# A matmul with bias and residual: x transposed by VectorE in 32 x 32 blocks of word pairs, instead of by TensorE

## The chip, the cores and the metric

The kernel runs on one core of a Trainium2 chip. The time is device time in microseconds; the kernel before takes 211.29 us (median of three runs, 211.21 to 211.32). Engines are named as the profile names them: PE (TensorE; PEld is its weight load), DVE (VectorE), ACT (ScalarE), POOL (GpSimd) and SP (SyncE, whose queue issues nearly all DMAs here).

## The reference

```python
# x: (16, 512, 1024), weight: (1024, 768), bias: (768,), residual: (16, 512, 768), all float32
return (np.matmul(x, weight) + bias + residual).astype(np.float32)
```

As two-dimensional arrays x is 8192 x 1024, the weights 1024 x 768 and the result 8192 x 768. The kernel multiplies in bf16 and adds in float32.

## The kernel before, in words

The 8192 rows are 64 tiles of 128 rows, in eight groups of G = 8 tiles. A group is loaded whole: partition p gets eight consecutive rows (4 MB of x, 3 MB of residual), and tile j of the group is row j of each partition. x has two slots of a group (`x_tile`); residuals, results and the staged weights share four homes of 3 MB (`home`, in the order of `HOME`).

A tile t goes through these steps:

- `cast_x(t)` (L120): ACT casts the 128 x 1024 tile to bf16, `xb`. It runs three tiles ahead.
- `transpose(t)` (L135): TensorE multiplies eight 128 x 128 pieces of `xb` with an identity into PSUM, `pt`. Piece (h, j) takes every fourth column of a half.
- `copy_xt(t)` (L142): DVE copies `pt` to SBUF, `xt`.
- `matmul(t)` (L149): for each of eight k, one matmul of 512 and one of 256 columns, into `po` in PSUM (three buffers).
- `evacuate(t)` (L163, L166): DVE adds `po` to the residual in place, and POOL adds the bias (L173). In group 0 the residual is not there yet: DVE adds the bias into `o_tile`, and POOL (two of them DVE) later adds the residual (L177).

The order on each engine is the program's order (`keep_in_program_order`). In the main loop PE does the transposes of tile t + 1 and then the product of tile t. All loads of x and residual and all stores are issued from the SP queue in program order; the table `moves` says behind which tile each one stands. An issue waits until its buffer is free and, because there are eight DMA semaphores in turn, until the eighth DMA before it has landed; whatever stands behind it on SP waits too. Ahead of the loop the weights come in four pieces, cast by ACT and DVE alternately, and 14 matmuls on constants (`fill`, L199) keep PE running while the first data arrive. The last tile is done in two column chunks and stored in two pieces.

Of the kernel before, what the change touches and what calls it, by code (L numbers as in the profile page):

```python
# [8 lines left out]
FP32 = mybir.dt.float32  # L9
BF16 = mybir.dt.bfloat16  # L10
P = 128
G = 8
X_BUFS = 2
HOME = [3, 1, 0, 3, 1, 2, 0, 3]
XB_BUFS = 5
XT_BUFS = 4
PT_BUFS = 2
PO_BUFS = 3
# [3 lines left out]
def kernel(  # L22
# [8 lines left out]
    nc = tc.nc  # L31
# [5 lines left out]
    n_k = K // P  # L37
    n_sub = M // P
    n_grp = n_sub // G
    chunks = [(0, 512), (512, N - 512)]  # L40

    def group(ap, g):

        return ap[g * G * P:(g + 1) * G * P, :].rearrange("(p j) k -> p j k", p=P)


    w_dram = weight.rearrange("(h p j) n -> h p j n", p=P, j=4)

# [5 lines left out]
    pt_pool = ctx.enter_context(  # L54
        tc.tile_pool(name="ptp", bufs=1, space=bass.MemoryType.PSUM))
# [3 lines left out]
    def o(ins):  # L59
        return tc.keep_in_program_order(ins)  # L60
# [7 lines left out]


    warm_in = const.tile([P, P], BF16, name="warm_in")  # L70
    o(nc.vector.memset(warm_in, 0.5))
# [5 lines left out]
    ident = const.tile([P, P], BF16, name="ident")  # L77
    make_identity(nc, ident)
    w_sb = const.tile([P, n_k, N], BF16, name="w_sb")
    bias_bc = const.tile([P, N], FP32, name="bias_bc")  # L80

    def home(i, name):
        return ring_pool.tile([P, G, N], FP32, name=name, tag=f"ring{i}", bufs=1)


    x_tiles, r_tiles, o_tiles, w_stage = {}, {}, {}, {}
# [6 lines left out]
    def load_w(h, j0, j1):  # L93
        if not w_stage:
            w_stage[0] = home(0, "w_stage")
        o(nc.sync.dma_start(out=w_stage[0][:, 4 * h + j0:4 * h + j1, :],
                            in_=w_dram[h, :, j0:j1, :]))

    def load_r(g):
        r_tiles[g] = home(HOME[g], "r_tile")  # L100
        o(nc.sync.dma_start(out=r_tiles[g], in_=group(res2d, g)))

    def store(g, j0=0, j1=G, n0=0, n1=N):
        src = o_tiles[g] if g == 0 else r_tiles[g]
        o(nc.sync.dma_start(out=group(out2d, g)[:, j0:j1, n0:n1], in_=src[:, j0:j1, n0:n1]))


    xb_tiles, pt_tiles, xt_tiles, po_tiles = {}, {}, {}, {}

    def cast_x(t, split=False):  # L110
        if t >= n_sub:
            return
        xb_tiles[t] = slot(xb_pool, "xb", XB_BUFS, [P, K], BF16)
        src = x_tiles[t // G][:, t % G, :]
        if split:
            h = K // 2
            o(nc.scalar.copy(out=xb_tiles[t][:, :h], in_=src[:, :h]))  # L117
            o(nc.vector.tensor_copy(out=xb_tiles[t][:, h:], in_=src[:, h:]))  # L118
        else:
            o(nc.scalar.copy(out=xb_tiles[t], in_=src))  # L120

    def cast_w(k, act=False):
        if act:
            o(nc.scalar.copy(out=w_sb[:, k, :], in_=w_stage[0][:, k, :]))  # L124
        else:
            o(nc.vector.tensor_copy(out=w_sb[:, k, :], in_=w_stage[0][:, k, :]))  # L126

    def transpose(t):
        if t >= n_sub:
            return  # L130
        xb = xb_tiles.pop(t).rearrange("m (h p j) -> m h j p", p=P, j=4)
        pt = slot(pt_pool, "pt", PT_BUFS, [P, n_k, P], BF16)
        for k in range(n_k):
            h, j = divmod(k, 4)
            o(nc.tensor.transpose(out=pt[:, k, :], in_=xb[:, h, j, :], identity=ident))  # L135
        pt_tiles[t] = pt

    def copy_xt(t):
        if t >= n_sub:
            return  # L140
        xt_tiles[t] = slot(xt_pool, "xt", XT_BUFS, [P, n_k, P], BF16)
        o(nc.vector.tensor_copy(out=xt_tiles[t], in_=pt_tiles.pop(t)))  # L142

    def matmul(t, k0=0, k1=n_k):
        if t not in po_tiles:
            po_tiles[t] = slot(po_pool, "po", PO_BUFS, [P, N], FP32)
        for k in range(k0, k1):
            for (n0, nl) in chunks:
                o(nc.tensor.matmul(  # L149
                    po_tiles[t][:, n0:n0 + nl],  # L150
                    lhsT=xt_tiles[t][:, k, :],
                    rhs=w_sb[:, k, n0:n0 + nl],
                    start=(k == 0),
                    stop=(k == n_k - 1),
                ))

    def evacuate(t):


        g, j = divmod(t, G)  # L160
        po = po_tiles.pop(t)
        if g == 0:
            o(nc.vector.tensor_add(out=o_tiles[0][:, j, :], in0=po, in1=bias_bc))  # L163
        else:
            rt = r_tiles[g][:, j, :]
            o(nc.vector.tensor_add(out=rt, in0=po, in1=rt))  # L166
            if t < n_sub - 3:
                add_bias(t)
        xt_tiles.pop(t)

    def add_bias(t, engine=nc.gpsimd):
        rt = r_tiles[t // G][:, t % G, :]
        o(engine.tensor_add(out=rt, in0=rt, in1=bias_bc))  # L173

    def add_residual(t, engine=nc.gpsimd):
        ot = o_tiles[0][:, t, :]
        o(engine.tensor_add(out=ot, in0=ot, in1=r_tiles[0][:, t, :]))  # L177


    load_x(0, 0, 2)  # L180
    load_w(0, 0, 2)
    load_x(0, 2, 4)
    for q, n0, n1 in [(0, 0, 512), (0, 512, N), (32, 0, N), (64, 0, N), (96, 0, N)]:
        o(nc.scalar.dma_start(out=bias_rows[q:q + 1, n0:n1], in_=bias[None, n0:n1]))  # L184
    load_w(0, 2, 4)
    load_w(1, 0, 2)
    load_w(1, 2, 4)
    load_x(0, 4, 6)
    load_x(0, 6, 8)
# [3 lines left out]


    warm_ps = po_pool.tile([P, 4, P], FP32, name="warm_ps", tag="po2", bufs=1)

    def fill(n):
        for i in range(n):
            o(nc.tensor.matmul(warm_ps, lhsT=warm_in,  # L199
                               rhs=warm_in[:, None, :].to_broadcast([P, 4, P]),  # L200
                               start=True, stop=True))


    fill(11)
    cast_x(0, True)
    transpose(0)
    fill(2)
    copy_xt(0)
    cast_x(1)
    cast_w(0, True)  # L210
    transpose(1)
    copy_xt(1)
    cast_w(1)
    fill(1)
    matmul(0, 0, 1)
    matmul(1, 0, 1)
    matmul(0, 1, 2)
    matmul(1, 1, 2)
    cast_x(2, True)
    transpose(2)  # L220
    copy_xt(2)
    matmul(2, 0, 2)
    for k in range(2, 6):
        cast_w(k, k % 2 == 0)
        for t in range(3):
            matmul(t, k, k + 1)
    o(nc.vector.stream_shuffle(out=bias_bc, in_=bias_rows, mask=[0] * 32))  # L227
    cast_w(6)
    cast_w(7, True)
    cast_x(3, True)  # L230
    matmul(0, 6, 8)
    evacuate(0)
    transpose(3)
    matmul(1, 6, 8)
    copy_xt(3)
    matmul(2, 6, 8)
    evacuate(1)
    evacuate(2)
    cast_x(4)
    cast_x(5)  # L240
# [3 lines left out]
        4: [(load_x, 2)],  # L244
        5: [(load_r, 0), (load_r, 2)],
        12: [(load_x, 3)],
        15: [(store, 1)],
        17: [(load_r, 3)],
        20: [(load_x, 4)],
        21: [(load_r, 4), (store, 0)],  # L250
        28: [(load_x, 5)],
        29: [(load_r, 5), (store, 2)],
        36: [(load_x, 6)],
        37: [(load_r, 6), (store, 3)],
        44: [(load_x, 7)],
        45: [(load_r, 7), (store, 4)],
        47: [(store, 5)],
        55: [(store, 6)],
        59: [(store, 7, 0, 4)],
        61: [(store, 7, 4, 6)],  # L260
        62: [(store, 7, 6, 7)],
    }
    for t in range(3, n_sub - 1):
        cast_x(t + 3)
        if t == 3:
            matmul(t, 0, 5)
            transpose(t + 1)
            matmul(t, 5, 8)
        elif t == G - 1:
            matmul(t, 0, 2)  # L270
            transpose(t + 1)
            matmul(t, 2, 8)
        else:
            transpose(t + 1)
            matmul(t)
        copy_xt(t + 1)
        if t in (2 * G, 2 * G + 1):
            add_residual(t - 2 * G, nc.vector)
        evacuate(t)
        if t in (n_sub - 9, n_sub - 7, n_sub - 5):  # L280
            add_bias(n_sub - 3 + (t - n_sub + 9) // 2)
        if t == 2 * G - 1:
            for u in range(2, G):
                add_residual(u)
        for move, *what in moves.get(t, []):
            move(*what)


    t = n_sub - 1
    for (n0, nl) in chunks:  # L290
        ps = slot(po_pool, "po", PO_BUFS, [P, nl], FP32, name="last_ps")
        for k in range(n_k):
            o(nc.tensor.matmul(ps, lhsT=xt_tiles[t][:, k, :], rhs=w_sb[:, k, n0:n0 + nl],  # L293
                               start=(k == 0), stop=(k == n_k - 1)))
        rt = r_tiles[n_grp - 1][:, G - 1, n0:n0 + nl]
        o(nc.vector.tensor_add(out=rt, in0=ps, in1=rt))  # L296
        store(n_grp - 1, G - 1, G, n0, n0 + nl)
# [28 lines left out]
```

## Time and profile before

| | before |
|---|---|
| median of 3 runs | 211.29 us (211.21 to 211.32) |
| the profiled execution | 210.92 us, with a span of 209.1 us |
| granted TensorE clock | 1.000 |
| moved by DMA | 87.28 MB, 417 GB/s over the span |
| PE / DVE / ACT / POOL busy | 199.5 / 107.3 / 67.7 / 114.4 us |
| waits of POOL for DVE's sums | 85.2 us |
| SP's waits on POOL before stores | 54.8 us, 3 times |

The span runs from the first to the last instruction of the profiled execution; the time of the execution is 1.82 us longer. Busy time counts the instructions of an engine, with matmuls modelled as pipelined. A row of the groups reads: line, engine, operation, output<-input with shapes, count, then busy time and mean duration in ns, then the idle time just before and what ended it. A row of the windows reads: stretch and length, busy time (and instructions) of PE, PEld, DVE, ACT and POOL, then the granted clock, the share of time in which the DMA engines were busy, and GB/s.

### The profile page before, as it was taken

To read this page: it belongs to the slowest core of one execution; us is meant where nothing else is said; L and a number is where in the kernel's file an instruction comes from. 1 tells how busy PE (TensorE), PEld (TensorE's weight loads), DVE (VectorE), ACT (ScalarE), POOL (GpSimd) and SP (SyncE) were. 2 spreads that over 40 slices of the span, in tenths; PEclk is the share of its full clock that TensorE was granted. 3 is DMA by queue.
4 is the path that set the end of the run, shared out by engine and by line. 5 is a ranking of instruction groups with operands and counts; after the bars stand their busy time and mean duration, and the time that the engine had idled before them with its cause. 6 is when DMAs were issued, how large, how long until landed. Compare 5 with 4: busy or idle time off the path is not lost.

```text
span 209.1 us, 3593 instructions
## 1 busy us (share of the span) xinstructions
PE 199.5 (95%) x1520; PEld 130.8 (63%) x1550; DVE 107.3 (51%) x142; ACT 67.7 (32%) x70; POOL 114.4 (55%) x69
## 2 busy tenths in 40 slices
PE   7679999999999999999999999999999999999992
PEld 2346766666666666666666666666666666666661
DVE  0457555455478545454554554455445445544542
ACT  2446309507331074303632063310733018320000
POOL 2000000365579999966556655655665565599820
PEclk9999999999999999999999999999999999999999
DMA  6999999999999999999999999999999999999994
GB/s 241 416 424 445 461 418 412 464 400 437 431 453 396 418 439 395 454 445 414 431 431 445 418 414 451 434 426 429 417 432 431 461 409 423 417 434 442 409 385 192
DMA packets 5066, 87.28 MB, mean 417 GB/s; under 512 B 565, under 2 KB 694, under 8 KB 1594
## 3 DMA queue, kind: packets, MB, share of 16 engines
q1 hardware_dynamic: 5040, 87.03, 97.8%
q8 instruction: 12, 0.20, 0.4%
q14 instruction: 4, 0.03, 0.0%
q10 hardware_dynamic: 10, 0.01, 0.0%
HBM read 61.88 MB, written 25.17 MB: 416 GB/s over the span
## 4 chain that ended last, share of the span: by engine, by line
PE 82%; DMA 14%; ACT 1%; issue 1%; SPq 0%; DVE 0%; ACTq 0%
PE po L149 69%; PE pt L135 12%; DMA x_tile<-in_x_dram 11%; DMA bias_rows<-in_bias_dram 2%; PE last_ps L293 1%; ACT L76 1%; ACT xb L120 1%; SPq L91 0%; DVE r_tile L296 0%; ACT warm L76 0%; ACTq L120 0%; ACTq L184 0%
## 5 line engine op out<-in xcount | busy, mean ns | idle before, releaser
L149 PE MATMUL po<-w_sb,xt 128*128 128x256 bf16 (+1 forms) x978 | 172.1, 324 | 2.6 <-DVE xt L142 0.8
L173 POOL TENSOR_TENSOR r_tile<-r_tile,bias_bc 128x768 f32<-128x768 f32 x56 | 101.0, 1814 | 85.2 <-DVE r_tile L166 85.2
L149 PEld LDWEIGHTS <-xt 128*128 128x128 bf16 x1008 | 95.8, 98 | 58.9 <-DVE xt L142 1.4
L120 ACT CAST xb<-x_tile 128x1024 bf16<-128x1024 f32 x61 | 61.2, 1044 | 108.5 <-DMA x_tile<-in_x_dram 64.6
L166 DVE TENSOR_TENSOR r_tile<-po,r_tile 128x768 f32<-128x768 f32 x55 | 52.7, 958 | 79.1 <-PE po L149 73.2
L142 DVE COPY xt<-pt 128x1024 bf16<-128x1024 bf16 x64 | 43.6, 682 | 3.1 <-PE pt L135 3.1
L135 PEld LDWEIGHTS <-xb 128*128 128x128 bf16 x512 | 35.4, 113 | 11.0 <-ACT xb L117 3.0
L135 PE MATMUL pt<-ident,xb 128*128 128x128 bf16 x512 | 39.1, 219 | 2.2 <-ACT xb L117 2.2
L177 POOL TENSOR_TENSOR o_tile<-o_tile,r_tile 128x768 f32<-128x768 f32 x6 | 12.1, 2056 | 0.0
L163 DVE TENSOR_TENSOR o_tile<-po,bias_bc 128x768 f32<-128x768 f32 x8 | 7.6, 955 | 7.0 <-PE po L149 7.0
L199 PE MATMUL warm_ps<-warm_in 128*128 128x512 bf16 x14 | 5.3, 530 | 1.0 <-DVE warm L75 1.0
L124 ACT CAST w_sb<-w_stage 128x768 bf16<-128x768 f32 x4 | 3.3, 832 | 3.7 <-DMA w_stage<-in_weight_dram 3.7
L118 DVE CAST xb<-x_tile 128x512 bf16<-128x512 f32 x3 | 1.3, 424 | 6.0 <-DMA x_tile<-in_x_dram 6.0
L199 PEld LDWEIGHTS <-warm_in 128*128 128x128 bf16 x14 | 1.7, 131 | 3.4 <-issue 2.4
L117 ACT CAST xb<-x_tile 128x512 bf16<-128x512 f32 x3 | 1.8, 615 | 5.6 <-DMA x_tile<-in_x_dram 5.6
L177 DVE TENSOR_TENSOR o_tile<-o_tile,r_tile 128x768 f32<-128x768 f32 x2 | 3.3, 1647 | 0.0
L126 DVE CAST w_sb<-w_stage 128x768 bf16<-128x768 f32 x4 | 2.2, 556 | 1.7 <-DMA w_stage<-in_weight_dram 1.7
L293 PE MATMUL last_ps<-w_sb,xt 128*128 128x512 bf16 (+1 forms) x16 | 2.8, 326 | 0.0
L293 PEld LDWEIGHTS <-xt 128*128 128x128 bf16 x16 | 1.6, 98 | 1.1
L296 DVE TENSOR_TENSOR r_tile<-last_ps,r_tile 128x512 f32<-128x512 f32 (+1 forms) x2 | 1.1, 558 | 0.9 <-PE last_ps L293 0.8
L76 ACT ACT_TABLE_LOAD x1 | 1.3, 1283 | 0.7 <-PEq L310 0.7
L227 DVE STREAM_SHUFFLE bias_bc<-bias_rows 128x768 f32<-128x768 f32 x1 | 1.0, 1006 | 0.0
(11 smaller groups left out, 2.1 us busy)
## 6 DMA issues: line engine op xcount, KB each, us to landing
x_tile<-in_x_dram SPq DMA_DIRECT2D x7, 4096.0 KB, 29.2
r_tile<-in_residual_dram SPq DMA_DIRECT2D x8, 3072.0 KB, 17.7
out_dram<-r_tile SPq DMA_DIRECT2D x6, 3072.0 KB, 23.9
x_tile<-in_x_dram SPq DMA_DIRECT2D x4, 1024.0 KB, 8.8
w_stage<-in_weight_dram SPq DMA_DIRECT2D x4, 768.0 KB, 6.5
out_dram<-o_tile SPq DMA_DIRECT2D x1, 3072.0 KB, 31.2
out_dram<-r_tile SPq DMA_DIRECT2D x1, 1536.0 KB
out_dram<-r_tile SPq DMA_DIRECT2D x1, 768.0 KB, 5.5
```

The lines of the kernel that those rows point to most:

```text
L76: o(nc.scalar.copy(out=warm, in_=warm))
L120: o(nc.scalar.copy(out=xb_tiles[t], in_=src))
L124: o(nc.scalar.copy(out=w_sb[:, k, :], in_=w_stage[0][:, k, :]))
L135: o(nc.tensor.transpose(out=pt[:, k, :], in_=xb[:, h, j, :], identity=ident))
L142: o(nc.vector.tensor_copy(out=xt_tiles[t], in_=pt_tiles.pop(t)))
L149: o(nc.tensor.matmul(po_tiles[t][:, n0:n0 + nl], lhsT=xt_tiles[t][:, k, :], rhs=w_sb[:, k, n0:n0 + nl], start=(k == 0), stop=(k == n_k - 1),))
L163: o(nc.vector.tensor_add(out=o_tiles[0][:, j, :], in0=po, in1=bias_bc))
L166: o(nc.vector.tensor_add(out=rt, in0=po, in1=rt))
L173: o(engine.tensor_add(out=rt, in0=rt, in1=bias_bc))
L177: o(engine.tensor_add(out=ot, in0=ot, in1=r_tiles[0][:, t, :]))
L199: o(nc.tensor.matmul(warm_ps, lhsT=warm_in, rhs=warm_in[:, None, :].to_broadcast([P, 4, P]), start=True, stop=True))
L293: o(nc.tensor.matmul(ps, lhsT=xt_tiles[t][:, k, :], rhs=w_sb[:, k, n0:n0 + nl], start=(k == 0), stop=(k == n_k - 1)))
```

## The change

TensorE no longer transposes. `xb` is seen as 32-bit words, each a pair of neighbouring bf16 values, and DVE transposes 32 x 32 blocks of such words. Work goes by batches of B = 4 tiles. The columns of x are split in four quarters q of 256 (128 words); word 4a + j of quarter q is to land on partition 32q + a, so that partition p holds columns 8p to 8p + 7, and the weights are loaded accordingly in one DMA, partition p holding rows 8p to 8p + 7. A transposed block comes out on the 32 partitions its rows were on (m), and must move to the 32 partitions of its quarter (q):

- Quarters 0 and 1: DVE transposes all 128 partitions in one instruction into `tq` (`transpose_blocks`), and ACT moves the blocks in four copies of 32 partitions each (`move_blocks`).
- Quarters 2 and 3: DVE transposes each 32 partitions with an instruction of its own that also writes them to their place (`transpose_and_move`, four instructions).

The product reads every second bf16 of `xt` as weights. There are two `xt` and four `po`; each `xb` quarter and `tq` has one buffer. The identity, the PSUM tiles for transposes, the warming matmuls, the split of the first casts and of the last tile go. All eight residual adds of group 0 are on POOL. The last residual group is loaded into a slot of x, and the order of homes and `moves` is new, now by batches.

The diff, cut to its core:

```diff
-    def transpose(t):
-        xb = xb_tiles.pop(t).rearrange("m (h p j) -> m h j p", p=P, j=4)
-        pt = slot(pt_pool, "pt", PT_BUFS, [P, n_k, P], BF16)
-        for k in range(n_k):
-            h, j = divmod(k, 4)
-            o(nc.tensor.transpose(out=pt[:, k, :], in_=xb[:, h, j, :], identity=ident))
-        pt_tiles[t] = pt
-    def copy_xt(t):
-        xt_tiles[t] = slot(xt_pool, "xt", XT_BUFS, [P, n_k, P], BF16)
-        o(nc.vector.tensor_copy(out=xt_tiles[t], in_=pt_tiles.pop(t)))
+    def load_r(g):
+        if g == n_grp - 1:
+            xs = slot(xin_pool, "x_tile", X_BUFS, [P, G * K], FP32, name="r_last")
+            r_tiles[g] = xs[:, :G * N].rearrange("p (j n) -> p j n", n=N)
+        else:
+            r_tiles[g] = home(HOME[g], "r_tile")
+        o(nc.sync.dma_start(out=r_tiles[g], in_=group(res2d, g)))
+    def cast_x(b, q):
+        g, j = divmod(b * B, G)
+        xb = slot(xb_pool, f"xb{q}_", 1, [P, B, KQ], BF16)
+        o(nc.scalar.copy(out=xb, in_=x_tiles[g][:, j:j + B, q * KQ:(q + 1) * KQ]))
+        xb_tiles[b, q] = xb.bitcast(U32).rearrange("p t (a j) -> p t j a", j=R // 2)
+    def xt_tile(b):
+        if b not in xt_tiles:
+            xt_tiles[b] = slot(xt_pool, "xt", 2, [P, B, R // 2, P], U32)
+        return xt_tiles[b]
+    def transpose_blocks(b, q):
+        tq_tiles[b, q] = slot(xt_pool, f"tq{q}_", 1, [P, B, R // 2, Q], U32)
+        o(nc.vector.transpose(out=tq_tiles[b, q], in_=xb_tiles.pop((b, q))))
+    def move_blocks(b, q):
+        xt, tq = xt_tile(b), tq_tiles.pop((b, q))
+        for m in range(P // Q):
+            o(nc.scalar.copy(out=xt[q * Q:(q + 1) * Q, :, :, m * Q:(m + 1) * Q],
+                             in_=tq[m * Q:(m + 1) * Q]))
+    def transpose_and_move(b, q):
+        xt, xb = xt_tile(b), xb_tiles.pop((b, q))
+        for m in range(P // Q):
+            o(nc.vector.transpose(out=xt[q * Q:(q + 1) * Q, :, :, m * Q:(m + 1) * Q],
+                                  in_=xb[m * Q:(m + 1) * Q]))
     def matmul(t):
+        b, i = divmod(t, B)
+        xt = xt_tiles[b].bitcast(BF16)[:, i].rearrange("p j (m r) -> p j r m", r=2)
...
-                    lhsT=xt_tiles[t][:, k, :],
+                    lhsT=xt[:, k // 2, k % 2, :],
...
+    load_x(0, 0, B)
+    w_stage = home(3, "w_stage")
+    o(nc.sync.dma_start(out=w_stage, in_=weight.rearrange("(p r) n -> p r n", p=P)))
+    load_x(0, B, G)
+    load_x(1)
+    load_r(1)
...
+    load_x(2)
+    load_r(0)
+    load_r(2)
+    moves = {
+        1: [(load_x, 3)],
+        3: [(load_x, 4), (load_r, 3)],
+        4: [(store, 1)],
+        5: [(load_x, 5), (load_r, 4), (store, 0)],
+        7: [(load_x, 6), (load_r, 5), (store, 2)],
+        9: [(load_x, 7), (load_r, 6)],
+        11: [(load_r, 7), (store, 3), (store, 4)],
+        12: [(store, 5)],
+        14: [(store, 6)],
+    }
+    for b in range(n_bat):
+        t = B * b
+        matmul(t)
+        for q in (0, 1):
+            transpose_blocks(b + 1, q)
+        evacuate(t - 1)
+        for q in (0, 1):
+            move_blocks(b + 1, q)
+        for q in range(4):
+            if q < 2:
+                cast_x(b + 2, q)
+        matmul(t + 1)
+        transpose_and_move(b + 1, 2)
+        evacuate(t)
+        cast_x(b + 2, 2)
+        matmul(t + 2)
+        transpose_and_move(b + 1, 3)
+        evacuate(t + 1)
+        cast_x(b + 2, 3)
+        matmul(t + 3)
+        evacuate(t + 2)
+        if b in (2, 3):
+            for u in range(B * (b - 2), B * (b - 1)):
+                add_residual(u)
...
+        if b == n_bat - 1:
+            store(n_grp - 1, 0, B)
+        for move, *what in moves.get(b, []):
+            move(*what)
+    evacuate(n_sub - 1)
+    store(n_grp - 1, B, B + 2)
+    store(n_grp - 1, B + 2, G)
```

In the text below, x3 or r3 is the load of x or of the residual for group 3.

More of the change, by code (lines that the diff above doesn't have):

```diff
@@ L5 @@
 from concourse import mybir
-from concourse.masks import make_identity
 from concourse._compat import with_exitstack
@@ L10 @@
 BF16 = mybir.dt.bfloat16
+U32 = mybir.dt.uint32
 P = 128
+Q = 32
 G = 8
+B = 4
 X_BUFS = 2
[L14 to L18, printed above, removed]
+HOME = [0, 1, 3, 0, 1, 2, 3]
+PO_BUFS = 4
 @with_exitstack
@@ L36 @@
     N = weight.shape[1]
-    n_k = K // P
+    R = K // P
+    KQ = K // 4
     n_sub = M // P
     n_grp = n_sub // G
+    n_bat = n_sub // B
     chunks = [(0, 512), (512, N - 512)]
@@ L44, in group @@
         return ap[g * G * P:(g + 1) * G * P, :].rearrange("(p j) k -> p j k", p=P)
-    w_dram = weight.rearrange("(h p j) n -> h p j n", p=P, j=4)
     const = ctx.enter_context(tc.tile_pool(name="const", bufs=1))
@@ L53 @@
     xt_pool = ctx.enter_context(tc.tile_pool(name="xtp", bufs=1))
-    pt_pool = ctx.enter_context(
-        tc.tile_pool(name="ptp", bufs=1, space=bass.MemoryType.PSUM))
     po_pool = ctx.enter_context(
@@ L67, in slot, with home @@
         return pool.tile(shape, dtype, name=name or base, tag=f"{base}{i % n}", bufs=1)
-    warm_in = const.tile([P, P], BF16, name="warm_in")
-    o(nc.vector.memset(warm_in, 0.5))
+    def home(i, name):
+        return ring_pool.tile([P, G, N], FP32, name=name, tag=f"ring{i}", bufs=1)
     bias_rows = const.tile([P, N], FP32, name="bias_rows")
@@ L76 @@
     o(nc.scalar.copy(out=warm, in_=warm))
-    ident = const.tile([P, P], BF16, name="ident")
-    make_identity(nc, ident)
-    w_sb = const.tile([P, n_k, N], BF16, name="w_sb")
+    w_sb = const.tile([P, R, N], BF16, name="w_sb")
     bias_bc = const.tile([P, N], FP32, name="bias_bc")
-    def home(i, name):
-        return ring_pool.tile([P, G, N], FP32, name=name, tag=f"ring{i}", bufs=1)
-    x_tiles, r_tiles, o_tiles, w_stage = {}, {}, {}, {}
+    x_tiles, r_tiles, o_tiles = {}, {}, {}
     def load_x(g, j0=0, j1=G):
@@ L91, in load_x @@
         o(nc.sync.dma_start(out=x_tiles[g][:, j0:j1, :], in_=group(x2d, g)[:, j0:j1, :]))
[L93 to L97, printed above, removed]
-    def load_r(g):
-        r_tiles[g] = home(HOME[g], "r_tile")
+    def load_r(g):
+        if g == n_grp - 1:
[3 more added lines that the diff above has]
+            r_tiles[g] = home(HOME[g], "r_tile")
@@ L101, in load_r, with store @@
         o(nc.sync.dma_start(out=r_tiles[g], in_=group(res2d, g)))
-    def store(g, j0=0, j1=G, n0=0, n1=N):
+    def store(g, j0=0, j1=G):
         src = o_tiles[g] if g == 0 else r_tiles[g]
[L105 to L111, printed above, removed]
+        o(nc.sync.dma_start(out=group(out2d, g)[:, j0:j1, :], in_=src[:, j0:j1, :]))
+    xb_tiles, tq_tiles, xt_tiles, po_tiles = {}, {}, {}, {}
@@ L112, in cast_x @@
+    def cast_x(b, q):
+        if b >= n_bat:
             return
[L113 to L126, printed above, removed]
@@ L128, in transpose @@
-    def transpose(t):
-        if t >= n_sub:
-            return
-        xb = xb_tiles.pop(t).rearrange("m (h p j) -> m h j p", p=P, j=4)
-        pt = slot(pt_pool, "pt", PT_BUFS, [P, n_k, P], BF16)
-        for k in range(n_k):
-            h, j = divmod(k, 4)
-            o(nc.tensor.transpose(out=pt[:, k, :], in_=xb[:, h, j, :], identity=ident))
-        pt_tiles[t] = pt
-    def copy_xt(t):
-        if t >= n_sub:
-            return
-        xt_tiles[t] = slot(xt_pool, "xt", XT_BUFS, [P, n_k, P], BF16)
-        o(nc.vector.tensor_copy(out=xt_tiles[t], in_=pt_tiles.pop(t)))
@@ L144, in matmul @@
[L144 to L147, printed above, removed]
+        g, j = divmod(b * B, G)
[6 more added lines that the diff above has]
+        return xt_tiles[b]
@@ new lines, in transpose_blocks @@
+    def transpose_blocks(b, q):
+        if b >= n_bat:
+            return
+        tq_tiles[b, q] = slot(xt_pool, f"tq{q}_", 1, [P, B, R // 2, Q], U32)
+        o(nc.vector.transpose(out=tq_tiles[b, q], in_=xb_tiles.pop((b, q))))
+    def move_blocks(b, q):
+        if b >= n_bat:
+            return
+        xt, tq = xt_tile(b), tq_tiles.pop((b, q))
+        for m in range(P // Q):
+            o(nc.scalar.copy(out=xt[q * Q:(q + 1) * Q, :, :, m * Q:(m + 1) * Q],
+                             in_=tq[m * Q:(m + 1) * Q]))
@@ new lines, in transpose_and_move, with matmul @@
+    def transpose_and_move(b, q):
+        if b >= n_bat:
+            return
+        xt, xb = xt_tile(b), xb_tiles.pop((b, q))
+        for m in range(P // Q):
+            o(nc.vector.transpose(out=xt[q * Q:(q + 1) * Q, :, :, m * Q:(m + 1) * Q],
+                                  in_=xb[m * Q:(m + 1) * Q]))
+    def matmul(t):
+        b, i = divmod(t, B)
+        xt = xt_tiles[b].bitcast(BF16)[:, i].rearrange("p j (m r) -> p j r m", r=2)
+        po_tiles[t] = slot(po_pool, "po", PO_BUFS, [P, N], FP32)
+        for k in range(R):
@@ L150, in matmul @@
                     po_tiles[t][:, n0:n0 + nl],
-                    lhsT=xt_tiles[t][:, k, :],
+                    lhsT=xt[:, k // 2, k % 2, :],
                     rhs=w_sb[:, k, n0:n0 + nl],
                     start=(k == 0),
-                    stop=(k == n_k - 1),
+                    stop=(k == R - 1),
                 ))
     def evacuate(t):
+        if t < 0:
+            return
         g, j = divmod(t, G)
@@ L166, in evacuate, with add_bias, add_residual @@
             o(nc.vector.tensor_add(out=rt, in0=po, in1=rt))
-            if t < n_sub - 3:
+            if t < n_sub - 2:
                 add_bias(t)
-        xt_tiles.pop(t)
-    def add_bias(t, engine=nc.gpsimd):
+    def add_bias(t):
         rt = r_tiles[t // G][:, t % G, :]
-        o(engine.tensor_add(out=rt, in0=rt, in1=bias_bc))
-    def add_residual(t, engine=nc.gpsimd):
+        o(nc.gpsimd.tensor_add(out=rt, in0=rt, in1=bias_bc))
+    def add_residual(t):
         ot = o_tiles[0][:, t, :]
[L177 to L189, printed above, removed]
+        o(nc.gpsimd.tensor_add(out=ot, in0=ot, in1=r_tiles[0][:, t, :]))
+    for p in range(0, P, Q):
+        o(nc.scalar.dma_start(out=bias_rows[p:p + 1, :], in_=bias[None, :]))
+    load_x(0, 0, B)
+    w_stage = home(3, "w_stage")
+    o(nc.sync.dma_start(out=w_stage, in_=weight.rearrange("(p r) n -> p r n", p=P)))
+    load_x(0, B, G)
     load_x(1)
@@ L192 @@
     o_tiles[0] = home(2, "o_tile")
[L195 to L240, printed above, removed]
-    moves = {
[L244 to L261, printed above, removed]
-    }
@@ L263 @@
[L263 to L278, printed above, removed]
-        evacuate(t)
[L280 to L283, printed above, removed]
-                add_residual(u)
-        for move, *what in moves.get(t, []):
-            move(*what)
@@ L289 @@
[L289 to L297, printed above, removed]
+    o(nc.vector.stream_shuffle(out=bias_bc, in_=bias_rows, mask=[0] * 32))
@@ new lines @@
+    for q in range(4):
+        cast_x(0, q)
+    for q in (0, 1):
+        transpose_blocks(0, q)
+    for q in (2, 3):
+        transpose_and_move(0, q)
+    for q in (0, 1):
+        move_blocks(0, q)
+    for k in range(R):
+        if k % 2:
+            o(nc.scalar.copy(out=w_sb[:, k, :], in_=w_stage[:, k, :]))
+        else:
+            o(nc.vector.tensor_copy(out=w_sb[:, k, :], in_=w_stage[:, k, :]))
+    for q in range(4):
+        cast_x(1, q)
+    load_x(2)
+    load_r(0)
+    load_r(2)
@@ new lines @@
+    moves = {
+        1: [(load_x, 3)],
[7 more added lines that the diff above has]
+        14: [(store, 6)],
+    }
+    for b in range(n_bat):
+        t = B * b
+        matmul(t)
+        for q in (0, 1):
+            transpose_blocks(b + 1, q)
+        evacuate(t - 1)
+        for q in (0, 1):
+            move_blocks(b + 1, q)
+        for q in range(4):
+            if q < 2:
+                cast_x(b + 2, q)
+        matmul(t + 1)
+        transpose_and_move(b + 1, 2)
+        evacuate(t)
+        cast_x(b + 2, 2)
[7 more added lines that the diff above has]
+            for u in range(B * (b - 2), B * (b - 1)):
+                add_residual(u)
+        if b == n_bat - 3:
+            for u in (n_sub - 2, n_sub - 1):
+                add_bias(u)
+        if b == n_bat - 1:
+            store(n_grp - 1, 0, B)
+        for move, *what in moves.get(b, []):
+            move(*what)
```

## The prediction

> **What bounds the kernel now.** I read the engine and DMA lines of the page first.
>
> ```profile
> PE 199.5 (95%) x1520; PEld 130.8 (63%) x1550; DVE 107.3 (51%) x142; ACT 67.7 (32%) x70; POOL 114.4 (55%) x69
> DMA  6999999999999999999999999999999999999994
> DMA packets 5066, 87.28 MB, mean 417 GB/s; under 512 B 565, under 2 KB 694, under 8 KB 1594
> PE 82%; DMA 14%; ACT 1%; issue 1%; SPq 0%; DVE 0%; ACTq 0%
> ```
>
> Two resources are full at once: TensorE is busy 95% of the span, and the DMA engines are busy in every slice but the first and the last. The chain names PE only because a transfer that arrives in time leaves no wait behind. So I asked for the rates by stretch.
>
> ```profile
> 0.00:6.00 6.00, 4.29 (x11) 1.45 (x11) 0.44 (x3) 1.75 (x3) 1.38 (x7) 1.00 0.70 259
> 6.00:12.00 6.00, 4.01 (x35) 2.25 (x35) 2.61 (x6) 2.74 (x4) 0.00 (x0) 1.00 1.01 419
> ...
> 125.00:150.00 25.00, 24.79 (x194) 16.56 (x196) 12.67 (x17) 8.80 (x9) 15.11 (x9) 1.00 1.00 429
> ...
> 200.00:209.10 9.10, 5.40 (x36) 3.12 (x34) 3.54 (x5) 0.00 (x0) 0.14 (x1) 1.00 0.67 271
> ```
>
> The last two columns are DMA share and GB/s. From 6 to 200 us the share is 1.00 and the weighted rate of all the stretches is 429 GB/s (83.26 MB in 194 us). The first 6 us move 1.55 MB, worth 3.6 us at that rate, and lose 2.4; the last 9.1 us move 2.47 MB, worth 5.75, and lose 3.35. All of the span is then 87.28 MB / 429 = 203.4, plus 2.4, plus 3.35 = 209.1 us. The change moves the same bytes, so freeing TensorE can win back only what lies in the 3.35. Everything else can only be lost. That is the main point of this forecast. Then the groups and two rows of the timeline give durations.
>
> ```profile
> L166 DVE TENSOR_TENSOR r_tile<-po,r_tile 128x768 f32<-128x768 f32 x55 | 52.7, 958 | 79.1 <-PE po L149 73.2
> L142 DVE COPY xt<-pt 128x1024 bf16<-128x1024 bf16 x64 | 43.6, 682 | 3.1 <-PE pt L135 3.1
> L117 ACT CAST xb<-x_tile 128x512 bf16<-128x512 f32 x3 | 1.8, 615 | 5.6 <-DMA x_tile<-in_x_dram 5.6
> L227 DVE STREAM_SHUFFLE bias_bc<-bias_rows 128x768 f32<-128x768 f32 x1 | 1.0, 1006 | 0.0
> L177 DVE TENSOR_TENSOR o_tile<-o_tile,r_tile 128x768 f32<-128x768 f32 x2 | 3.3, 1647 | 0.0
> 35.73 2.60 PE po L149 x16
> 38.33 0.45 PE pt L135 x8
> ```
>
> A tile is 2.60 us of product and 0.45 us of transpose on PE, a period of 3.05.
>
> **TensorE, step by step.** The 512 transposes go: 64 x 0.45 = 29 us. What stays is 64 x 2.60 = 166 us, 10.4 us for a batch of four tiles. The weights of the product are now read with a step of two bf16 words. The trace has a longer step already: L135 loads xb with a step of four words, eight loads in 0.56 us, 70 ns each, while the shorter of the two matmuls of a k lasts 108 (a third of the 325 ns pair). I price the step at nothing. The 14 warming matmuls go too; the first tile may then run slowly for 2 to 3 us, which DMA hides.
>
> **VectorE.** It loses 43.6 us of copies (L142) and some smaller things. It gains, for each batch, two 128 x 512 block transposes and eight of 32 x 512, all of 32-bit words. No row shows a block transpose. The nearest is the shuffle, 1006 ns for 768 words. Two DVE widths of the same add (692 ns for 512, 425 for 256) differ by 1.04 ns a word, so the shuffle is 800 ns of streaming and 206 fixed, and a 512-word transpose 533 + 206 = 0.74 us. Lower end: 0.69, the 512-wide add. Upper end, from the slowest DVE row, L177: (1647 - 206) / 768 = 1.88 ns a word, 1.17 us. I take 0.74, since the shuffle is the row that also moves data between partitions. Two adds back to back on DVE take 1.81 us where their durations sum to 1.91, so the wide pair gets 1.4. The narrow ones each start in another group of 32 partitions, and I give them no overlap: 8 x 0.74 = 5.9. Four evacuations are 3.8. A batch is 11.1 us of DVE, more than PE's 10.4 but less than the 12.7 us that DMA needs for a sixteenth of its 203.4. DVE passes DMA when a transpose takes 0.9 us.
>
> **ScalarE.** Four casts of 1.04 and eight moves of 512 words by L117's 0.615: 4.2 + 4.9 = 9.1 us a batch. It has 2 us of cover under DVE. Its last cast of a batch waits for the last transposes of the batch ahead; behind it on the queue stand the moves of the next batch, which wait for two transposes that come 2.6 us later anyway.
>
> **Start.** The first x load is now 2.1 MB and ends at about 2.4 + 4.9 + 0.8 = 8.1 us, weights at 15.4. Casts 8.1 to 12.1, DVE transposes to about 17, weight casts to 20: the products begin near 17.5 instead of 8.5. The second batch is transposed by about 30, the third by 41, then one each 11.1 us: the sixteenth starts at 41 + 13 x 11.1 = 185, and its last tile is evacuated at 197 if nothing waits. That is before DMA can be done. The late start costs nothing while loads are queued: 14.7 MB are issued without a wait, which keeps DMA busy until 37 us, and the next 10.5 MB are released by the casts of the first eight tiles, near 25.
>
> **The SP queue.** I followed it as first come, first served at 429 GB/s (4.19 MB 9.8 us, 3.15 MB 7.3). x3 ends at 71, x4 (released at 64) at 81. Next is r3, which reuses the home of r0, and r0 is free when POOL has added all eight residual rows. POOL's adds of rows 0 to 3 stand behind tiles 8 to 10 (ready at 49 to 55), and take 4 x 2.06; then four bias adds of 1.81 and four more residual adds. That ends at 80 to 83 us; behind the waiting r3 on SP stand the store of group 1 and x5. The queue runs dry at 81, and from the first issue to first data the trace has about 1.7 us (0.73 to 2.4). I charge 1.9 us of idle DMA, between nothing and 5. In the kernel before, two of these residual adds ran on DVE. After that the releases come 5 to 14 us ahead of need (x5 at 86 for 96, x6 at 108 for 120, x7 at 130 for 145, r7 at 152 for 162). r6 arrives at about 163, some 5 us after its first evacuation could run; this delays compute to about 200, still hidden by stores that are queued until 206.
>
> **End.** Before, the last add ended at 205.9 and the span at 209.1. With the queue full until its last byte, the end loses the landing alone; I take 2.5 of the 3.35.
>
> **Sum.** 203.4 + 2.4 + 2.5 + 1.9 = 210.2 us of span. The profiled execution took 210.92 around a span of 209.1, 1.8 outside it; the median of the runs, 211.29, is 0.4 above that. So I expect 210.2 + 2.2 = 212.4 us, slower by half a percent.
>
> **Rivals.** *DMA never starves.* POOL finishes by 79, the 1.9 vanishes, and the span is 208.3, the time 210.5: faster by 0.4%. For it: before, DMA stayed at 1.00 through three stalls of SP on POOL (54.8 us in all). Against it: the margin here is 1 or 2 us. It decides by when POOL's eighth residual add ends, with 79 us as the point.
>
> *VectorE becomes the bound.* The block transpose reads xb with a step of four 32-bit words, 16 bytes; no DVE row of the trace reads with a step. If a step of that length halves the stream, a transpose takes 206 + 2 x 533 = 1.27 us, a batch 8 x 1.27 + 2.4 + 3.8 = 16.4. The first two batches' narrow transposes and the start of the third come 10 to 12 us later than 41, so the sixteenth batch starts near 52 + 13 x 16.4 = 265, and with 10.4 of product, 1 of evacuation, 3 of store the span is 279, the time 281. By L177's 1.17 us it is 8 x 1.17 + 2.1 + 3.8 = 15.3 a batch, 50 + 13 x 15.3 = 249 for the sixteenth, and 265. Against it: the stepped weight loads of L135 take 113 ns where the dense ones take 98; as a factor on the stream that is 0.82 us, 11.9 a batch, still under DMA.
> The Trainium skill, "Advanced Engine Details and Errata", section "SBUF Cachelines", says of 16-byte lines "Different cacheline per access: performance penalty" without a figure, and this step touches a new line with each word. By it the time would be this rival's if the penalty is a halving; no run here shows it.
>
> *ScalarE's moves are dearer than its casts.* At 0.95 us a move, ScalarE would need 11.8 a batch, still covered by DMA; it decides from 1.07.
>
> **Chances.** DVE at half rate 0.18 (265 to 281). Otherwise DMA sets the pace, 0.82: unstarved 0.26, at 209.0 to 210.9; 0.10 within 0.2% of 211.29; starved for some us, or with DVE at 11.7 to 13 us a batch, 0.46, at 211.7 to 228 (13 us a batch ends at 41 + 2 + 13 x 13 + 14.4 = 226). About 0.2% is what a measurement of this kernel can tell from no change. So faster 0.26, same 0.10, slower 0.64. The range leaves out the half-rate case and 0.02 below: 209.0 to 228. Within 0.82, the DMA-paced case by itself has 209 to 217.
>
> **What will show it.** In the profile of the changed kernel: DMA still at 9 in nearly all slices and near 429 GB/s with a total near 87.3 MB; PE at about 166 us busy or a little more, with waits for xt; the row of the narrow transposes at 0.70 to 0.82 us; DVE at 170 to 185 us busy, ACT near 150. SP waits on POOL o_tile before r3 at 80 to 83 us, with a dent in the DMA slice there. A transpose row above 0.9 us, DVE as the main share of the chain and DMA slices at 6 or 7 would make the forecast wrong, as would the DMA rate moving by more than 1% (2 us).

## The result, and the profile after

The changed kernel takes 261.56 us (median of 4 runs, 259.97 to 261.63) against 211.31 for the kernel before, a ratio of 1.236 (95% interval 1.231 to 1.241). The forecast was 212.4 us within 209 to 228; the time came out near that of the rival in which VectorE becomes the bound. The profiled execution took 261.61 us, with a span of 259.8. Its page, in the lines that answer to those shown of before (engines, DMA by slice, DMA total, chain by engine):

```profile
PE 185.9 (72%) x1024; PEld 104.5 (40%) x1024; DVE 234.1 (90%) x231; ACT 147.0 (57%) x198; POOL 116.0 (45%) x69
...
DMA  7999999999802999979985999869902999962855
...
DMA packets 4053, 87.22 MB, mean 336 GB/s; under 512 B 452, under 2 KB 452, under 8 KB 712
...
DVE 73%; issue 14%; PE 7%; DMA 3%; ACT 1%; ACTq 0%; DVEq 0%
```

DVE has taken the chain. The same bytes move at 336 GB/s in place of 417, with slices in which DMA does almost nothing, the shape that was said to prove the forecast wrong. One batch in the middle, from the windows (columns as before), and two batches of PE from the timeline (start, length, count, and in brackets the idle time before and what ended it):

```profile
127.50:142.20 14.70, 12.26 (x62) 6.65 (x61) 14.49 (x15) 8.92 (x12) 7.25 (x5) 0.85 0.85 323
```

```profile
125.19 12.24 PE L147 MATMUL po<-w_sb,xt 128*128 128x512 bf16 x64 [4.11 <-DVE xt L138]
139.87 12.24 PE L147 MATMUL po<-w_sb,xt 128*128 128x512 bf16 x64 [2.44 <-DVE xt L138]
```

A batch lasts 14.7 us, and DVE is busy for 14.5 of them. PE waits for each `xt`, in most batches 2 to 4 us. From the second batch at 37.3 us to the sixteenth at 242.4 there are 14 periods of 14.65. The groups of DVE say which instruction it is (mean ns behind the comma; the third row is a wide transpose from the rows of its line, with min/median/max in ns):

```profile
L138 DVE STREAM_TRANSPOSE xt<-xb__845 32x512 uint32<-32x512 uint32 x4 | 4.5, 1122 | 0.1
L166 DVE TENSOR_TENSOR r_tile<-po,r_tile 128x768 f32<-128x768 f32 x48 | 44.2, 942 | 0.8
...
L122 DVE STREAM_TRANSPOSE tq__908<-xb__818 x1: 1096/1096/1096, 126.8 to 126.8; 128x512 uint32<-128x512 uint32 x1
```

The narrow transposes take 1.07 to 1.14 us where 0.74 was forecast, the wide ones 1.04 to 1.12. Eight at 1.1, two at 1.0 (start to start) and four evacuations at 0.93 (also start to start) make 8.8 + 2.0 + 3.7 = 14.5, all of the batch. The waits of SP show how DVE starves DMA: `xb` has one buffer a quarter, so ACT's last cast waits for DVE's last transposes, and a load into that slot of x waits for that cast (L83 loads x; L92 here loads the last residual, which takes a slot of x). Us in total, times, longest:

```profile
SPq L83 <- ACT xb__541 L109: 28.9, 1, 28.9
SPq L92 <- ACT xb__1404 L109: 28.4, 1, 28.4
SPq L83 <- ACT xb__1190 L109: 27.9, 1, 27.9
```

The first of these waits ends at 82 us, and the slice in which nothing moves, 71.4 to 77.9 us, lies within it.

What stays open after this reading is why a transpose takes 1.1 us.

### The profile page after: what moved, and what is told of

It is laid out like the page before. It is cut to its first block, busy times and chain, and to the rows that moved or that the text cites. A ratio compares the mean times of both kernels' runs of the same rounds, so it can differ in the third digit from the quotient of the medians.

```text
span 259.8 us, 2757 instructions
## 1 busy us (share of the span) xinstructions
PE 185.9 (72%) x1024; PEld 104.5 (40%) x1024; DVE 234.1 (90%) x231; ACT 147.0 (57%) x198; POOL 116.0 (45%) x69
## 4 chain that ended last, share of the span: by engine, by line
DVE 73%; issue 14%; PE 7%; DMA 3%; ACT 1%; ACTq 0%; DVEq 0%
DVE xt L138 43%; DVE r_tile L166 14%; PE po L147 7%; DMA bias_rows<-in_bias_dram 3%; DVE o_tile L163 2%; DVE r_last L166 1%; DVE w_sb L201 1%; ACT L73 0%; DVE tq__803 L122 0%; DVE tq__1337 L122 0%; DVE tq__1123 L122 0%; DVE tq__1552 L122 0%; DVE tq__474 L122 0%; DVE bias_bc L188 0%; DVE tq__1018 L122 0%
## 5 line engine op out<-in xcount | busy, mean ns | idle before, releaser
L147 PE MATMUL po<-w_sb,xt 128*128 128x512 bf16 (+1 forms) x1024 | 185.9, 347 | 68.7 <-DVE xt L138 44.8
L147 PEld LDWEIGHTS <-xt 128*128 128x128 bf16 x1024 | 104.5, 103 | 149.7 <-issue 65.9
L172 POOL TENSOR_TENSOR r_tile<-r_tile,bias_bc 128x768 f32<-128x768 f32 x48 | 86.6, 1818 | 131.9 <-DVE r_tile L166 130.8
L166 DVE TENSOR_TENSOR r_tile<-po,r_tile 128x768 f32<-128x768 f32 x48 | 44.2, 942 | 0.8
L172 POOL TENSOR_TENSOR r_last<-r_last,bias_bc 128x768 f32<-128x768 f32 x8 | 14.3, 1813 | 4.0 <-DVE r_last L166 3.9
L176 POOL TENSOR_TENSOR o_tile<-o_tile,r_tile 128x768 f32<-128x768 f32 x8 | 14.3, 1813 | 0.0
L166 DVE TENSOR_TENSOR r_last<-po,r_last 128x768 f32<-128x768 f32 x8 | 7.5, 955 | 7.0 <-PE po L147 6.9
L109 ACT CAST xb__95<-x_tile 128x1024 bf16<-128x1024 f32 x1 | 1.0, 1044 | 6.4 <-DMA x_tile<-in_x_dram 6.4
L138 DVE STREAM_TRANSPOSE xt<-xb__1379 32x512 uint32<-32x512 uint32 x4 | 4.5, 1128 | 0.1
L138 DVE STREAM_TRANSPOSE xt<-xb__516 32x512 uint32<-32x512 uint32 x4 | 4.5, 1124 | 0.1
L138 DVE STREAM_TRANSPOSE xt<-xb__845 32x512 uint32<-32x512 uint32 x4 | 4.5, 1122 | 0.1
L138 DVE STREAM_TRANSPOSE xt<-xb__950 32x512 uint32<-32x512 uint32 x4 | 4.5, 1122 | 0.1
L138 DVE STREAM_TRANSPOSE xt<-xb__735 32x512 uint32<-32x512 uint32 x4 | 4.5, 1121 | 0.1
L138 DVE STREAM_TRANSPOSE xt<-xb__407 32x512 uint32<-32x512 uint32 x4 | 4.5, 1120 | 0.1
L138 DVE STREAM_TRANSPOSE xt<-xb__629 32x512 uint32<-32x512 uint32 x4 | 4.5, 1116 | 0.1
L138 DVE STREAM_TRANSPOSE xt<-xb__1488 32x512 uint32<-32x512 uint32 x4 | 4.5, 1115 | 0.1
L138 DVE STREAM_TRANSPOSE xt<-xb__1594 32x512 uint32<-32x512 uint32 x4 | 4.4, 1111 | 0.1
L138 DVE STREAM_TRANSPOSE xt<-xb__1060 32x512 uint32<-32x512 uint32 x4 | 4.4, 1110 | 0.1
L138 DVE STREAM_TRANSPOSE xt<-xb__1165 32x512 uint32<-32x512 uint32 x4 | 4.4, 1109 | 0.1
L138 DVE STREAM_TRANSPOSE xt<-xb__1274 32x512 uint32<-32x512 uint32 x4 | 4.4, 1109 | 0.1
```

The source lines that it names most:

```text
L109: o(nc.scalar.copy(out=xb, in_=x_tiles[g][:, j:j + B, q * KQ:(q + 1) * KQ]))
L138: o(nc.vector.transpose(out=xt[q * Q:(q + 1) * Q, :, :, m * Q:(m + 1) * Q], in_=xb[m * Q:(m + 1) * Q]))
L147: o(nc.tensor.matmul(po_tiles[t][:, n0:n0 + nl], lhsT=xt[:, k // 2, k % 2, :], rhs=w_sb[:, k, n0:n0 + nl], start=(k == 0), stop=(k == R - ...
L172: o(nc.gpsimd.tensor_add(out=rt, in0=rt, in1=bias_bc))
L176: o(nc.gpsimd.tensor_add(out=ot, in0=ot, in1=r_tiles[0][:, t, :]))
```

## The experiments

My theory S was that the 16-byte step of the read is what costs. Its rivals were W, that a transpose of 32-bit words streams at about two cycles a word whatever the step, and F, a large fixed cost per transpose. For the period itself the rival was that the order of waits between DVE and ACT sets it, and not DVE's sum.

**The disputed row by itself (e0_rows).** For instance:

```diff
+    def words(t, step, n=W):
+        return t[:, :n].rearrange("p (t a j) -> p t j a", j=step, a=Q)
+    for i in range(4):
+        o(nc.vector.transpose(out=dst[i].rearrange("p (c j a) -> p c j a", j=4, a=Q), in_=words(su, 4)))
```

> The disputed row by itself. This kernel leaves out the matmul, bias and residual; it only runs DVE and ACT instructions four times each, and its span means nothing. In the changed kernel a block transpose of 512 words takes 1.04 to 1.13 us where 0.74 was forecast. Theory S (the 16-byte step of the read): with a step of one word 0.74 us, with two words between, with four words 1.1; a copy with a step of four slows too. Theory W (the word size): 1.1 us at every step, as a 32-bit transpose streams at about two cycles a word; a transpose of 16-bit elements takes 0.7. Theory F (a fixed cost of each transpose): 256 words take 0.8 us or more, against 0.55 to 0.6 by S and W.

The groups of this kernel. L67, L69 and L71 are wide transposes with a step of 1, 2 and 4 words, L73 and L75 of 256 words with 1 and 4, L77 and L79 narrow ones with 1 and 4, L81 of 16-bit elements, L83 and L85 DVE copies and L89 and L91 ACT copies with 1 and 4:

```profile
L79 DVE STREAM_TRANSPOSE dst<-src 32x512 uint32<-32x512 uint32 x4 | 4.3, 1066 | 0.1
L91 ACT COPY dstf<-src 128x512 f32<-128x512 f32 x4 | 4.0, 1082 | 0.0
L71 DVE STREAM_TRANSPOSE dst<-src 128x512 uint32<-128x512 uint32 x4 | 3.9, 1031 | 0.0
L77 DVE STREAM_TRANSPOSE dst<-src 32x512 uint32<-32x512 uint32 x4 | 2.8, 703 | 0.1
...
L81 DVE STREAM_TRANSPOSE dstb<-sb 128x512 bf16<-128x512 bf16 x4 | 2.5, 680 | 0.0
L67 DVE STREAM_TRANSPOSE dst<-src 128x512 uint32<-128x512 uint32 x4 | 2.5, 679 | 0.0
L89 ACT COPY dstf<-src 128x512 f32<-128x512 f32 x4 | 2.5, 618 | 25.0 <-DVE dstf L87 24.9
L69 DVE STREAM_TRANSPOSE dst<-src 128x512 uint32<-128x512 uint32 x4 | 2.4, 670 | 0.0
L85 DVE COPY dstf<-src 128x512 f32<-128x512 f32 x4 | 2.2, 606 | 0.0
L75 DVE STREAM_TRANSPOSE dst<-src 128x256 uint32<-128x256 uint32 x4 | 2.1, 580 | 0.0
L83 DVE COPY dstf<-src 128x512 f32<-128x512 f32 x4 | 1.4, 411 | 0.0
L73 DVE STREAM_TRANSPOSE dst<-src 128x256 uint32<-128x256 uint32 x4 | 1.4, 400 | 0.0
```

A dense transpose takes 0.68 us, one with a step of two words 0.67, one with four 1.03. W falls: 16-bit and 32-bit elements take the same 0.68. F falls: 256 words take 0.40. The slope from 256 to 512 words is (679 - 400) / 256 = 1.09 ns a word dense and (1031 - 580) / 256 = 1.76 stepped, 1.6 times as much and not twice. Copies pay as well: 0.61 us against 0.41 on DVE, 1.08 against 0.62 on ACT.

**The step taken out of the kernel (e1_step1).**

```diff
-        xb_tiles[b, q] = xb.bitcast(U32).rearrange("p t (a j) -> p t j a", j=R // 2)
+        xb_tiles[b, q] = xb.bitcast(U32).rearrange("p t (j a) -> p t j a", j=R // 2)
-    o(nc.sync.dma_start(out=w_stage, in_=weight.rearrange("(p r) n -> p r n", p=P)))
+    for q in range(4):
+        o(nc.sync.dma_start(
+            out=w_stage[q * Q:(q + 1) * Q].rearrange("a (j r) n -> a j (r n)", r=2),
+            in_=weight[q * KQ:(q + 1) * KQ, :].rearrange("(j a r) n -> a j (r n)", j=R // 2, r=2)))
```

> The changed kernel, with the words of a quarter dealt to partitions the other way round (word 32j + a on partition 32q + a), so that the transposes read with a step of one word; the weights are loaded in four DMAs of 32 partitions in the matching order. Theory S: a transpose takes 0.74 us, a batch 11.1 us of DVE, DMA sets the pace again, 208 to 216 us. Theory W: nothing changes on DVE, 14.6 us a batch, 258 to 264 us.

Measured: 217.47 us, 1.027 of the kernel before (1.024 to 1.031), a little above S's range and 44 us below the changed kernel. From its page (chain by engine) and its windows:

```profile
DMA 51%; PE 29%; DVE 7%; POOL 5%; issue 2%; ACT 1%; SPq 0%; DVEq 0%; ACTq 0%
```

```profile
6.00:12.00 6.00, 0.00 (x0) 0.00 (x0) 2.01 (x4) 3.53 (x4) 0.00 (x0) 1.00 1.02 269
12.00:20.00 8.00, 0.00 (x0) 0.10 (x1) 5.83 (x9) 5.19 (x9) 0.00 (x0) 1.00 1.03 208
20.00:30.00 10.00, 5.61 (x18) 2.56 (x18) 2.42 (x5) 4.56 (x6) 0.00 (x0) 1.00 1.03 371
```

DMA is back on the chain and DVE is off it. What is left over 210 is of the experiment's own making: the four weight loads of 32 partitions each keep the DMA engines busy at 208 to 269 GB/s. At 429 the three stretches would have moved 10.3 MB and moved 7.0, which is 7.7 us. The run e3 below bears this out.

**DVE relieved without touching the step (e2_act3).**

```diff
-        transpose_and_move(b + 1, 2)
+        transpose_blocks(b + 1, 2)
+        move_blocks(b + 1, 2)
         evacuate(t)
```

The same is done for batch 0, and quarter 2 shares the `tq` buffer of quarter 0.

> The changed kernel with the blocks of quarter 2 moved by ACT as those of quarters 0 and 1 are: DVE does three wide transposes and four narrow ones a batch instead of two and eight. If DVE's sum is the bound whatever the reason for its transposes (S, W or F): DVE 3 x 1.0 + 4 x 1.1 + 3.7 = 11.1 us a batch, ACT 12 moves in 7.5 and four casts in 3.8 = 11.3 us and some waits, so 11.5 to 12.5 us a batch and 215 to 228 us. If instead the order of waits between DVE and ACT sets the 14.6 us, about 255 to 262 us.

Measured: 223.02 us, 1.054 (1.050 to 1.058). Two batches of PE from its timeline:

```profile
133.12 10.58 PE L147 MATMUL po<-w_sb,xt 128*128 128x512 bf16 x64 [1.47 <-ACT xt L130]
145.12 10.57 PE L147 MATMUL po<-w_sb,xt 128*128 128x512 bf16 x64 [1.42 <-ACT xt L130]
```

The period is 12.0 us, as expected, and the wait of PE ends with ACT's moves. From 133.1 to 145.1 us DVE is busy for 11.1 us and ACT for 11.4; neither fills the period, so the waits between the two add some tenths here (chain: DVE 53%, ACT 24%, issue 12%). In the changed kernel DVE filled 14.5 of 14.7, and taking work from it shortened the period: it was DVE's sum, not the order of waits, that made the 14.7.

**The step halved, weights in one DMA (e3_step2).** With a step of two words the dense price holds, and the weights can be dealt so that one DMA fills all 128 partitions.

```diff
-        o(nc.scalar.copy(out=xb, in_=x_tiles[g][:, j:j + B, q * KQ:(q + 1) * KQ]))
-        xb_tiles[b, q] = xb.bitcast(U32).rearrange("p t (a j) -> p t j a", j=R // 2)
+        c = KQ // 2
+        src = x_tiles[g][:, j:j + B, :].rearrange("p t (h k) -> p t h k", h=2)
+        o(nc.scalar.copy(out=xb.rearrange("p t (h c) -> p t h c", h=2),
+                         in_=src[:, :, :, q * c:(q + 1) * c]))
+        xb_tiles[b, q] = xb.bitcast(U32).rearrange("p t (h a j) -> p (t h) j a", h=2, j=2)
-    o(nc.sync.dma_start(out=w_stage, in_=weight.rearrange("(p r) n -> p r n", p=P)))
+    o(nc.sync.dma_start(out=w_stage.rearrange("p (h j) n -> p h (j n)", h=2),
+                        in_=weight.rearrange("(h p j) n -> p h (j n)", h=2, p=P)))
```

> The changed kernel with a step of two words (8 bytes) in the transposes, and the weights again in one DMA over all 128 partitions: partition p holds columns 4p to 4p + 3 of each half of x, as in the kernel before, and a cast of a quarter reads two pieces of 128 columns. It has the dense transposes of e1 (0.67 and 0.70 us) without e1's weight loads at 203 to 304 GB/s, which lost about 7 us of DMA in its first 30 us. If DMA sets the pace, 217.5 - 7 = 210 to 211.5 us, so 0.992 to 1.001 of the kernel before. If DVE still sets it, 215 or more.

Measured: 209.79 us (209.22 to 210.14, 6 runs), 0.992 of the kernel before (0.990 to 0.994). This version beats both kernels, the one before by 0.8%, with an interval clear of 1. The transposes (narrow, then wide, min/median/max in ns), the page and the windows:

```profile
L142 DVE STREAM_TRANSPOSE xt<-xb__407 x4: 703/703/706, 55.4 to 57.6; 32x512 uint32<-32x512 uint32 x4
...
L125 DVE STREAM_TRANSPOSE tq__474<-xb__380 x1: 703/703/703, 53.2 to 53.2; 128x512 uint32<-128x512 uint32 x1
```

```profile
PE 173.8 (84%) x1024; PEld 101.6 (49%) x1024; DVE 171.1 (82%) x231; ACT 146.3 (70%) x198; POOL 115.3 (55%) x69
...
DMA  6999999999999999999999999999999999999995
...
DMA 53%; DVE 16%; PE 16%; POOL 5%; issue 4%; ACT 1%; SPq 1%; DVEq 0%; ACTq 0%
```

```profile
6.00:12.00 6.00, 0.00 (x0) 0.00 (x0) 2.38 (x5) 3.92 (x5) 0.00 (x0) 1.00 1.00 426
12.00:20.00 8.00, 1.79 (x6) 0.92 (x7) 7.42 (x12) 7.83 (x12) 0.00 (x0) 1.00 1.09 466
...
200.00:207.90 7.90, 0.29 (x2) 0.00 (x0) 0.96 (x1) 0.00 (x0) 0.00 (x0) 0.80 0.70 296
```

DMA is full from 6 to 200 us, and the span is 207.9. TensorE has 16% of idle time that buys nothing: its busy time fell from 199.5 us to 173.8, and what came of that is 1.6 us.

**Fewer bytes, on both sides (e4_step2_less, e5_before_less).** The same edit in e3 and in the kernel before:

```diff
-        o(nc.sync.dma_start(out=r_tiles[g], in_=group(res2d, g)))
+        if g != 3:
+            o(nc.sync.dma_start(out=r_tiles[g], in_=group(res2d, g)))
...
+        elif g == 3:
+            o(nc.vector.tensor_add(out=r_tiles[3][:, j, :], in0=po, in1=bias_bc))
```

> e3 without the load and the sum of group 3's residual (its rows get the bias alone): 3.15 MB less to move, 7.3 us at 429 GB/s. If DMA is what bounds e3, the time falls by 6 to 7.5 us, to about 203 to 205; if PE, DVE or the start bounds it, by less than 3.

> The kernel before, with the same left out (group 3's residual neither loaded nor added). If TensorE bounds that kernel as DMA does, the time falls by 0 to 2 us only, since 64 x 3.05 us of PE and its start stay; if DMA alone bounds it, by 6 to 7.5 us.

Without those 3.15 MB, e3 falls from 209.79 to 204.46 us (0.967 of the kernel before, 0.965 to 0.969), and the kernel before only from 211.36 to 210.40 (0.996, 0.994 to 0.997). The 5.3 us of e3 are a little under the 6 to 7.5 expected of a pure DMA bound. The chains, e4 first:

```profile
DMA 42%; PE 38%; DVE 9%; POOL 5%; issue 1%; ACT 1%; SPq 0%; ACTq 0%; DVEq 0%
```

```profile
PE 92%; DMA 4%; ACT 1%; DVE 1%; SPq 0%; issue 0%; ACTq 0%
```

So the kernel before was bound by PE and DMA at once, as the forecast had it, and e3 by DMA, with PE close behind.

**How the price grows with the step (e6_steps).**

```diff
+    tr(dst, su, 8)
+    tr(dst, su, 16)
+    tr16(4)
+    tr16(8)
```

> How the cost of a step grows. This kernel leaves out the matmul, bias and residual; it runs DVE and ACT instructions three times each, parted by memsets, and its span means nothing. In order on DVE: transposes of 32-bit words with a step of 1, 3 (480 words), 4, 8 and 16 words, of 16-bit elements with a step of 1, 4 and 8, copies of 512 words read densely and written with a step of four, adds with one input read with a step of four; then copies on ACT written with a step of four. If the price is that of a new 16-byte line with each word: 0.67, 0.63 to 0.85, 1.03, 1.03 and 1.03 us for the words, 0.67, 0.67 and 1.03 for the 16-bit elements. If it grows with the step: 8 and 16 words take more than 1.1. Writes: by the line as dear as reads (0.61 for the copy); otherwise 0.41.

The transposes in order of time, as rows of their line, each over its own stretch (min/median/max in ns). First words with a step of 1, 3, 4, 8 and 16:

```profile
L71 DVE STREAM_TRANSPOSE dst<-src x3: 653/661/669, 7.6 to 8.7; 128x512 uint32<-128x512 uint32 x3
L71 DVE STREAM_TRANSPOSE dst<-src x3: 714/769/772, 9.9 to 11.2; 128x480 uint32<-128x480 uint32 x3
L71 DVE STREAM_TRANSPOSE dst<-src x3: 954/1048/1048, 12.4 to 14.3; 128x512 uint32<-128x512 uint32 x3
L71 DVE STREAM_TRANSPOSE dst<-src x3: 968/1057/1058, 15.8 to 17.6; 128x512 uint32<-128x512 uint32 x3
L71 DVE STREAM_TRANSPOSE dst<-src x3: 919/1000/1001, 19.1 to 20.9; 128x512 uint32<-128x512 uint32 x3
```

Then 16-bit elements with a step of 4 and 8:

```profile
L76 DVE STREAM_TRANSPOSE dstb<-s x3: 664/673/680, 24.6 to 25.8; 128x512 bf16<-128x512 bf16 x3
L76 DVE STREAM_TRANSPOSE dstb<-s x3: 954/1042/1044, 26.9 to 28.7; 128x512 bf16<-128x512 bf16 x3
```

The price comes in full at 16 bytes and does not grow: 1.05, 1.06 and 1.00 us at 16, 32 and 64 bytes. At 12 bytes a part of it is there (0.77 us, where 480 dense words would take about 0.63), at 8 nothing. For 16-bit elements the step that costs is eight, again 16 bytes. A dense read written with such a step costs alike: 0.60 us for the DVE copy and 1.10 for the ACT copy, against 0.41 and 0.62 for the dense copies of e0. An add with one stepped input took 1.02; its dense counterpart was not run.

## Why the prediction was wrong

**The step that failed** is a single price: "533 + 206 = 0.74 us" for a transpose, with the sentence that took it "since the shuffle is the row that also moves data between partitions". For a dense read it is 0.67 to 0.71 (e0, e1), so the row was well chosen for the operation. But the transposes of the change read with a step of 16 bytes, and the row does not. They took 1.04 to 1.14, past the stated point of 0.9 at which DVE passes DMA, and each batch grew by 3.5 us over the 11.1 of the sum.

**Why I weighed it too low.** The rival had the mechanism, at 1.27 us and 281, or 1.17 and 265; the measured 1.1 and 261.6 lie just below. That 1.17 is so close is luck: it came from a dense add, L177, whose 1647 ns is the mean of two unlike instructions, 1104 and 2190. The rows of L177 in the kernel before (min/median/max in ns):

```profile
L177 POOL TENSOR_TENSOR o_tile<-o_tile,r_tile x6: 1813/1824/2532, 62.5 to 72.8; 128x768 f32<-128x768 f32 x6
L177 DVE TENSOR_TENSOR o_tile<-o_tile,r_tile x2: 1104/1647/2190, 61.2 to 64.7; 128x768 f32<-128x768 f32 x2
```

Against the rival I set the stepped weight loads, 113 ns for 98. Their step was four bf16, 8 bytes, and at 8 bytes a transpose pays nothing (0.67 in e0). Counted in bytes, that row was no evidence on a step of 16; I had counted it in elements.

The rule of 16-byte lines that the forecast quoted gave the better guess. The Trainium skill, "Advanced Engine Details and Errata", section "SBUF Cachelines", says that accesses which each fall in a different 16-byte line are penalised. The runs agree: the full price stands at steps of 16 bytes and more, 1.6 times a word, a part at 12 bytes, where three accesses in four meet a new line, and none at 8. That the line is the reason is the page's statement; the runs show the steps at which it costs.

**What held.** With the step down to 8 bytes, e3 comes nearest to the kernel that the forecast described. Its products begin at 18.2 us (forecast: near 17.5), DMA runs at about 429 GB/s from 6 to 200 us, and the span is 207.9, the rival "DMA never starves" (208.3, 210.5 us; measured 209.79). The 1.9 us charged for r3 were not lost: SP issued it at 77.5 us, before the 79 named as the point; the residual adds on POOL took 1.82 us and not 2.06, a mean that one add of 2.53 had raised (median 1.82, in the rows above). ACT's moves took 0.616 for 0.615. The weight loads at a step of two bf16 take 98 ns in the median, as dense ones did before, so pricing them at nothing was right. A batch of products takes 10.6 us, for 10.4.

**What I gave no weight.** In the changed kernel ten of the sixteen batches of products take 12.0 to 13.0 us in place of 10.6, at a granted clock of 0.93 over the run and 0.85 in the batch shown. The six batches that begin after a wait of about 4 us for `xt` are all among them, while in e2, from its fourth batch on, the waits are 1.5 us at most and all batches take 10.6. This suggests that the longer waits lower the clock; no run isolates it. The delay is hidden behind DVE in all batches but the last, which ends 1.7 us later for it.

## What to carry to other kernels

Price an access pattern by its step in bytes, from a row with the same step or a run that measures it: here one rearrangement, with the same instructions on the same engines, was worth 44 to 52 us. When a profile shows DMA full in every slice, work that is taken from the engine on the chain can return no more than the loss at the two ends (here 2.4 and 3.35 us, of which 1.6 came back); dropping some bytes in a run shows which of two full resources is the bound. Moving work to an engine with slack, as ACT had here (57% busy beside DVE's 90%), is a second way out, but it treats the symptom: e2 stops at 223 us, e3 at 210.

## What the runs showed of the hardware

Reading 512 elements that lie 16 bytes apart took 1.03 to 1.14 us in a DVE transpose (0.67 to 0.71 when they are dense or 8 bytes apart), 0.61 in a DVE copy (0.41 dense) and 1.08 in an ACT copy (0.62 dense). Transposes of 16-bit elements paid as those of 32-bit words did (1.04), and 64 bytes cost no more than 16 (1.00). Copies that write with this step took 0.60 on DVE and 1.10 on ACT; no run writes a transpose with a step.

Four DMAs of 32 partitions, queued one behind the other (e1), kept the engines' busy share at 1.0 while they moved only 208 to 269 GB/s, so a full busy share is not a full rate. The kernel before loads its weights in the same runs of two rows but over 128 partitions, and moved 419 GB/s from 6 to 12 us; so the length of the runs alone does not explain it. The 32 partitions are the likely reason, but no run isolates it.
